# Mixer and output of a hybrid decoder trunk: another order of the pooling maps, masks and shift as matmuls, output in pairs of tiles

## The chip, the core and the metric

The kernel runs on one core of a Trainium2 chip. The metric is the device time of one execution in microseconds (us); smaller is better. Five engines run their own instruction queues in order and wait for one another by semaphores: TensorE (PE in the profile; PEld is its weight load), VectorE (DVE), ScalarE (ACT), GpSimd (POOL) and SyncE (SP), which here only issues DMA transfers. Some transfers are issued from ACT's queue.

## The reference

One step of a trunk of two layers, for a prompt of 256 tokens and eight single tokens of other requests, side by side as 264 columns of width 1024. Each layer is feed-forward, mixer, feed-forward, each followed by a layer norm.

```python
h = layer_norm(DN_ALPHA * x + 0.5 * swiglu(x, f1g, f1u, f1d), ln1_g, ln1_b)
...
h = layer_norm(DN_ALPHA * h + mix, ln2_g, ln2_b)
y = layer_norm(DN_ALPHA * h + 0.5 * swiglu(h, f2g, f2u, f2d), ln3_g, ln3_b)
```

The mixer projects h to q, k, v, z, two gate rows and pooling inputs p. One half is a gated delta rule of four heads (causal convolution of width 4 and silu on q, k, v; decays as exp of differences of running sums, masked to the causal half; a triangular solve). The other half takes trailing means over 2, 4, 8 and 16 positions of four groups p(0) to p(3), minus the token, times a 128x128 matrix for each group. Outputs are the last hidden state and the new states.

## The kernel before

The hidden state X lies in SBUF as eight tiles of 128 features by 264 columns. Every large product is made of three matmuls for each of 8 slices (`mm3`, L217): each number is split into a rounded part and a rest, so weights exist as `whi` (ACT, L178) and `wlo` (DVE, L183, one instruction of 128x1024 for each product), and the state as HH and HL, or, before its norm is known, RH and RL. A product of 24 matmuls fills one 128x264 tile.

The order on PE is the order in which the code is written. On the other engines a scheduler orders the instructions, guided by `tc.high_priority()` and `behind(...)`. The in-order queue that results is what counts.

**Norms.** Class `Norm` (L239) sums X and its squares tile by tile on POOL or DVE (`acc`). `stats` (L337) makes mean and variance by four f32 matmuls `ps`; `normalise` (L357) subtracts and scales X in pairs of tiles. So that PE need not wait, `raw_products` (L401) first computes products of the unnormalised state (four k products `pk` in the mixer, six products in a feed-forward) with `stats` between them; `settle` corrects them afterwards (`fa`).

**Mixer, first part** (L495 on). After the four k products come `pba` (the two gate rows) together with the products q0 and p3, then `pbt` (transposes of the gates). DVE turns the gates into `bat`, a chain of small 128x12 instructions (L655 to L671), then `gm` (four 128x512 instructions, L702), which PE turns into `pdiff`, ACT into the decays `DT`, and POOL masks (L710, L711). Three functions make tiles: `q_tile` and `v_tile` (a product, then `conv`: one ACT and three DVE instructions `c`) and `p_tile` (L590: a product, a copy into `ext`, and on POOL g+1 sums `wsum`). `p_map(g)` (L609) makes the means `dm` by four DVE instructions, the last of them L620, and its `finish` the matmul `py` and a split into RH and RL. The order of these on PE is written out by hand: q1, p2, q2, p1, `py` of map 3, q3, the six `pdiff`, p0, `py` of map 2, v0, `py` of map 1, v1, v2, `py` of map 0, a mean (`centre`), v3.

`ext` and `wsum` have two buffers each, `dm` shares four buffers with others.

**Mixer, second part.** From `pP` on PE runs the levels of the triangular solve, with the decode tokens' state products `psk` and other work as fillers. `decode_conv` (L776) works on POOL and ACT; `less_shift` (L324) then subtracts a mean from all eight X tiles on POOL; `stack(0, ...)` (L902) makes `parts` on POOL (L906), which PE transposes (`pst`, L908). `s_read` (L854) scales the decode states S by their decay on POOL (L885). At last `w_pool` adds the output projection (`pop`, `pout`) to X.

**End.** `output` (L379) normalises the eight tiles on DVE, POOL and ACT, and SP writes them out.

Of the kernel before, what the change touches and what calls it, by code (L numbers as in the profile page):

```python
# [34 lines left out]
SB = 3  # L35
IDLE = 18
# [53 lines left out]
def trunk(ctx: ExitStack, tc: tile.TileContext, a: dict):  # L90
# [17 lines left out]
    gto = cpool.tile([P, 2, P], F32R, name="gto")  # L108

# [129 lines left out]
    class Norm:  # L239
# [52 lines left out]
        def add_scaled(self, m, ps, scale):  # L292
            y = X[:, m, :]
            if m >= 2:
                nc.vector.tensor_add(y, ps, y)
                self.shifted(m, nc.gpsimd, nc.gpsimd)
# [82 lines left out]
        def output(self, out):  # L379
            for m in (0, 1, 2, 3, 6, 7, 4, 5):  # L380
                y = X[:, m, :]
                (nc.gpsimd if m > 3 else nc.vector).tensor_sub(y, y, self.dmu)
            prev = None
            for m in (0, 1, 2, 3, 6, 4, 5, 7):
                y = X[:, m, :]
                if m > 5:
                    nc.gpsimd.tensor_mul(y, y, self.rstd)
                    with behind(prev):
                        nc.scalar.activation(y, y, AF.Identity, scale=self.g(m), bias=self.b(m))
                else:  # L390
                    nc.vector.scalar_tensor_tensor(y, y, self.g(m), self.rstd, ALU.mult, ALU.mult)
                    if m > 3:
                        nc.vector.tensor_scalar(y, y, self.b(m), None, ALU.add)
                    else:
                        prev = nc.scalar.activation(y, y, AF.Identity, bias=self.b(m))
                n = {4: 0, 6: 0, 5: 2, 7: 2}.get(m, 1)
                if n:
                    nc.sync.dma_start(out=out[(m - n + 1) * P:(m + 1) * P, :].rearrange("(m p) t -> p m t", p=P),
                                      in_=X[:, m - n + 1:m + 1, :])
# [28 lines left out]
    def ffn(src, norm, xnext, late=False):  # L428
        with tc.tile_pool(name="fp", bufs=1, reuse_waits="tile") as fp:
# [16 lines left out]
            if src is not None:  # L446
                W.ahead(6)
                raw = src.raw_products("gugugu", [((0,), 0, 6), ((1,), 0, 6), ((2,), 0, 6), None, ((3,), 0, 6),
# [46 lines left out]
    def mixer(l, src, norm, xstack):  # L495
        with tc.tile_pool(name="mp", bufs=1, reuse_waits="tile") as mp:
# [39 lines left out]
            def k_raw(ps):  # L536
                y, bias = src.settle(ps)
                raw = mp.tile([P, T], F32, name="raw", tag="tmp", bufs=4)
                nc.scalar.activation(raw, y, AF.Identity, bias=bias)
                return raw  # L540
# [5 lines left out]
            pk_ = src.raw_products("kkkk", [((0,), 0, 7), ((1,), 0, 7), None, ((0, 1), 7, KD), ((2,), 0, KD), ((3,), 0, KD)])  # L546
# [6 lines left out]
            pq, pp, pba = (psa.tile([P, T], F32, name=n, tag="ax") for n in ("pq", "pp", "pba"))  # L553
            for k in range(KD):
                nc.tensor.matmul(pba, wb[:, k, :], HH[:, k, :], start=k == 0, stop=False)
                nc.tensor.matmul(pba, wb[:, k, :], HL[:, k, :], start=False, stop=k == KD - 1)
                mm3(pq, wq, k, HH[:, k, :], HL[:, k, :], k == 0, k == KD - 1)
                mm3(pp, wp, k, HH[:, k, :], HL[:, k, :], k == 0, k == KD - 1)
            xstack.close()
# [6 lines left out]
            def q_tile(j, ps=None):  # L566
                W.ahead(2)
# [41 lines left out]
            def p_map(g):  # L609
                ext, smp, cur = pend[g]  # L610
                wd = 2 << g
                dm = mp.tile([P, T], F32, name="dm", tag="tmp", bufs=4)
# [9 lines left out]
                def finish():  # L622
                    py = psa.tile([P, T], F32, name="py", tag="ax")
                    nc.tensor.matmul(py, pw[:, g, :], dm, start=True, stop=True)
                    yp = mp.tile([P, T], F32, name="yp", tag="tmp", bufs=4)
# [5 lines left out]
            bar = mp.tile([8, 3 * P], F32, name="bar")  # L631
            nc.gpsimd.memset(bar[:, T:], 1.0)
            with tc.high_priority():
                nc.scalar.activation(bar[:, :T], pba[32:40], AF.Copy)
                nc.vector.tensor_add(bar[:, :T], pba[0:8], bar[:, :T])
            q_tile(0, pq)
            p_tile(3, pp)
            for j in range(4):
                conv(kr[j], j)
            ck = ct[0:4]  # L640

            pbt = psa.tile([P, 3, 8], F32, name="pbt", tag="ax")
            for t in range(3):
                nc.tensor.transpose(pbt[:, t, :], bar[:, t * P:(t + 1) * P], ident(8))
# [39 lines left out]

            q_tile(1)
            p_tile(2)
            q_tile(2)
            map3 = p_map(3)
# [3 lines left out]
            map2 = p_map(2)  # L692

# [4 lines left out]
            with tc.high_priority():  # L698
                for t in range(2):
                    for i in range(2):  # L700
                        gm = gms[t, i] = mp2.tile([P, H, P], F32R, name="gm", tag=f"{'TU'[t]}{i}")
                        nc.vector.tensor_mul(gm, lemask, gp[:, i, t, :].unsqueeze(2).to_broadcast([P, H, P]))  # L702
            for j, (t, msk) in enumerate(((0, gto[:, 1]), (1, gto[:, 0]), (1, gto[:, 1]))):
                pd = psa.tile([P, H, P], F32, name="pdiff", tag="ax")
                for i in range(2):
                    nc.tensor.matmul(pd, msk, gms[t, i], start=i == 0, stop=i == 1)
                dt = DT[:, :, j * P:(j + 1) * P]
                e_last = nc.scalar.activation(dt, pd, AF.Exp)
# [5 lines left out]
            p_tile(0)  # L714
            map2()
            v_tile(0, e_last)
            p_map(1)()
# [21 lines left out]
            for t in range(2):  # L739
                sumsq(ck, ssk, ke, t)  # L740
            v_tile(2, e_last)
# [4 lines left out]
            p_map(0)()  # L746
# [18 lines left out]

            state = {}
# [9 lines left out]
            def decode_conv():  # L776
# [9 lines left out]
                state["dsq"] = nc.gpsimd.tensor_mul(dsq[:, 8:12], dec[:, 0:4], dec[:, 4:8])  # L786
# [58 lines left out]
            skt = mp.tile([P, T], F32, name="skt", tag="tmp", bufs=4)[:, 0:P]  # L845
# [8 lines left out]
            def s_read(x):  # L854
# [18 lines left out]
                def last():  # L873
# [28 lines left out]
            def stack(i, src_, dst):  # L902
# [3 lines left out]
                nc.gpsimd.tensor_sub(pt[:, :, 2 - i, :], hb(src_), pt[:, :, 0, :])  # L906
                p = psa.tile([P, P], F32, name="pst", tag="ax")
# [47 lines left out]
            def w_pool(m):  # L955
# [6 lines left out]
                def step(k):  # L962
                    mm3(ps, w, 4 * (m % 2) + k, mh[4 + k], ml[4 + k], k == 0, k == 3)
# [108 lines left out]
            norm.less_shift(state["dsq"])  # L1072
# [15 lines left out]
            def stack_u():  # L1088
                stack(1, us, ust)
# [3 lines left out]
            def w_level():  # L1093
# [4 lines left out]
                       lambda: z_level(2, lambda: stack(0, dk, kst), s_read(1), nothing),  # L1098
# [179 lines left out]
    def constants_in():  # L1278
        nc.sync.dma_start(out=sm, in_=a["small"])
        nc.sync.dma_start(out=cst, in_=a["cst"])  # L1280
        nc.scalar.activation(onr, cst[:, C_M1024:C_M1024 + P], AF.Copy)
        nc.scalar.activation(gto, cst[:, C_ONE:C_ONE + 2 * P].rearrange("p (i n) -> p i n", i=2), AF.Copy)
# [107 lines left out]
```

## Time and profile before

| | |
|---|---|
| median of 3 runs | 1085.35 us (1083.95 to 1085.57) |
| profiled execution | 1089.43 us, of which the span is 1087.6 us |
| PE busy | 1046.0 us, 96% |
| DVE busy | 765.6 us, 70% |
| ACT busy | 581.8 us, 53% |
| POOL busy | 205.9 us, 19% |
| mean granted TensorE clock | 0.989 |

The profile shows one execution. Its shares are means over two feed-forwards and a mixer in each layer, which have different limits. A row of the waits view gives who waits on PE, for whom, the sum, how many times and the longest. A timeline row gives start, duration, engine, line, what is written and read, the count, and in brackets the idle time before it and who ended that. A duration contains the start-up of an instruction; the distance of two starts is what a queue advances.

### The profile page before, as it was taken

The numbers are of one execution on the slowest core, as the hardware profiler recorded it, in microseconds if no ns is written. First come the engines' busy times: TensorE is split into PE (matmuls) and PEld (weight loads), VectorE is DVE, ScalarE is ACT, GpSimd is POOL, SyncE is SP. The second block draws the span as 40 slices with busy tenths as digits, with TensorE's granted clock in tenths as the row PEclk, the third lists the DMA queues.
The fourth block names the chain that finished last, engine by engine and source line by source line (L and its number), as shares of the span: only waits on it lengthen the run. The fifth ranks groups of instructions, "written<-read, shape, count | busy, mean of one in ns | idle before, by whom it ended". The sixth has DMA issues, their size and how long they took to land.

```text
span 1087.6 us, 20766 instructions
## 1 busy us (share of the span) xinstructions
PE 1046.0 (96%) x8410; PEld 1030.9 (95%) x8410; DVE 765.6 (70%) x1226; ACT 581.8 (53%) x1016; POOL 205.9 (19%) x248
## 2 busy tenths in 40 slices
PE   8999999998899999999999999999899999999995
PEld 8999999988798999999999999999788999999994
DVE  5555567899789955557785555778996898555554
ACT  6444445666447744444574444466664476444432
POOL 0000012244940000003200000322467300000132
PEclk9999999999999999999999999999999999999997
DMA  8554444732234355544725545565331345455441
GB/s 306 187 192 172 179 172 184 290 130 83 97 133 169 127 190 189 194 169 180 265 86 194 179 172 192 180 236 195 130 119 41 154 165 188 166 190 194 155 156 40
DMA packets 35872, 183.24 MB, mean 168 GB/s; under 512 B 6848, under 2 KB 12608, under 8 KB 15552
## 3 DMA queue, kind: packets, MB, share of 16 engines
q1 hardware_dynamic: 28704, 175.19, 44.6%
q10 hardware_dynamic: 7072, 6.72, 1.8%
q8 instruction: 66, 1.08, 0.4%
q14 instruction: 30, 0.25, 0.1%
HBM read 175.18 MB, written 6.72 MB: 167 GB/s over the span
## 4 chain that ended last, share of the span: by engine, by line
PE 82%; DVE 10%; ACT 3%; POOL 2%; issue 1%; DMA 1%; ACTq 0%; DVEq 0%
PE pd L219 8%; PE pd L221 8%; PE pd L220 8%; PE pu L220 8%; PE pu L219 8%; PE pu L221 8%; PE pg L220 7%; PE pg L219 7%; PE pg L221 7%; DVE wlo L183 2%; POOL X L327 1%; DVE c L525 1%; ACT X L367 1%; DMA wraw<-in_f_gu 1%; PE pout L220 1%
## 5 line engine op out<-in xcount | busy, mean ns | idle before, releaser
L183 DVE TENSOR_TENSOR wlo<-wraw,whi 128x1024 fp32r<-128x1024 f32 (+1 forms) x301 | 369.9, 1231 | 203.8 <-ACT whi L178 203.0
L178 ACT ACTIVATE whi<-wraw 128x1024 fp32r<-128x1024 f32 (+1 forms) x301 | 312.5, 1041 | 318.7 <-issue 116.9
L219 PE MATMUL pd<-gh,whi 128*128 128x264 f32 x704 | 200.6, 285 | 0.0
L221 PE MATMUL pd<-gh,wlo 128*128 128x264 f32 x704 | 200.2, 284 | 0.0
L220 PE MATMUL pd<-gl,whi 128*128 128x264 f32 x704 | 199.1, 283 | 0.0
L219 PE MATMUL pg<-HH,whi 128*128 128x264 f32 x632 | 179.8, 284 | 1.2 <-ACT whi L178 1.2
L221 PE MATMUL pg<-HH,wlo 128*128 128x264 f32 x632 | 179.6, 284 | 0.3 <-DVE wlo L183 0.3
L219 PE MATMUL pu<-HH,whi 128*128 128x264 f32 x632 | 179.5, 284 | 0.0
L220 PE MATMUL pg<-HL,whi 128*128 128x264 f32 x632 | 179.4, 284 | 0.0
L220 PE MATMUL pu<-HL,whi 128*128 128x264 f32 x632 | 179.2, 284 | 0.0
L221 PE MATMUL pu<-HH,wlo 128*128 128x264 f32 x632 | 179.2, 284 | 0.0
L220 PEld LDWEIGHTS pd<-gl,whi 128*128 128x128 f32 x704 | 132.6, 188 | 0.0
L221 PEld LDWEIGHTS pd<-gh,wlo 128*128 128x128 f32 x704 | 132.6, 188 | 0.0
L219 PEld LDWEIGHTS pd<-gh,whi 128*128 128x128 f32 x704 | 132.5, 188 | 0.0
L301 POOL TENSOR_TENSOR s<-X 128x264 fp32r<-128x264 f32 x4 | 3.0, 759 | 632.7 <-DVE X L298 632.7
L219 PEld LDWEIGHTS pg<-HH,whi 128*128 128x128 f32 x632 | 119.1, 188 | 1.5 <-ACT whi L178 1.4
L221 PEld LDWEIGHTS pg<-HH,wlo 128*128 128x128 f32 x632 | 118.6, 188 | 0.9 <-DVE wlo L183 0.7
L220 PEld LDWEIGHTS pg<-HL,whi 128*128 128x128 f32 x632 | 119.2, 189 | 0.1
L220 PEld LDWEIGHTS pu<-HL,whi 128*128 128x128 f32 x632 | 119.2, 189 | 0.0
L219 PEld LDWEIGHTS pu<-HH,whi 128*128 128x128 f32 x632 | 119.1, 189 | 0.0
L221 PEld LDWEIGHTS pu<-HH,wlo 128*128 128x128 f32 x632 | 118.5, 188 | 0.0
L439 DVE TENSOR_TENSOR gt<-sg,pu 128x264 f32<-128x264 f32 x79 | 33.9, 429 | 50.5 <-PE pu L221 50.5
(374 smaller groups left out, 2051.0 us busy)
## 6 DMA issues: line engine op xcount, KB each, us to landing
wraw<-in_f_gu SPq DMA_DIRECT2D x86, 1024.0 KB, 4.8
wraw<-in_f_d SPq DMA_DIRECT2D x44, 1024.0 KB, 4.8
wraw<-in_w_in SPq DMA_DIRECT2D x20, 1024.0 KB, 5.0
wraw<-in_w_out SPq DMA_DIRECT2D x8, 1024.0 KB, 4.8
S<-in_sdelta SPq DMA_DIRECT2D x8, 512.0 KB, 6.2
out_o_ds<-S ACTq DMA_DIRECT2D x8, 512.0 KB, 2.6
X<-in_xT ACTq DMA_DIRECT2D x4, 264.0 KB, 5.4
wraw<-in_f_gu SPq DMA_DIRECT2D x4, 256.0 KB, 7.1
```

The costliest lines, as they stand in the source:

```text
L178: self.last_hi = nc.scalar.activation(h, r, AF.Copy)
L183: nc.vector.tensor_sub(l, r, h.bitcast(F32))
L219: nc.tensor.matmul(ps, hi[:, k, :], xh, start=first, stop=False)
L220: nc.tensor.matmul(ps, hi[:, k, :], xl, start=False, stop=False)
L221: nc.tensor.matmul(ps, lo[:, k, :], xh, start=False, stop=last)
L301: nc.gpsimd.tensor_add(self.s2, X[:, 0, :], X[:, 1, :])
L327: nc.gpsimd.tensor_sub(X[:, m, :], X[:, m, :], self.shift)
L367: nc.scalar.activation(X[:, m, :], X[:, m, :], AF.Identity, scale=self.g(m), bias=self.b(m))
L439: nc.vector.tensor_mul(gt, sg, u)
L525: nc.vector.scalar_tensor_tensor(c[:, d:SEQ], y[:, 0:SEQ - d], cw(j, 3 - d), c[:, d:SEQ], ALU.mult, ALU.add)
```

## The change

It has seven parts.

1. In `add_scaled` the last tile's instructions get high priority.
2. `stats` stands one product earlier in the mixer's `raw_products`, and one product later in the second feed-forward's (`late`).
3. `pba` runs beside q0 alone, and p3 follows; `pbt` is placed inside p3.
4. The convolutions of the four k products are spread between the q and p products, and the maps take another place: p0 is computed before `pdiff`, map 1 after v1, map 0 after v3. `dm` gets two buffers of its own.
5. POOL's masks on `DT` are replaced by matmuls that add a large negative number (`far`) above the diagonal, and by two further `pdiff` matmuls.
6. `less_shift` becomes a matmul of one row in each `pop` product; `parts` for `stack(0, ...)` is made right in `decode_conv`; S is scaled on ACT, in 128x128 pieces.
7. `output` works on pairs of tiles, reads the mean from PSUM on DVE, and issues four transfers instead of six.

```diff
@@ add_scaled
+                with tc.high_priority() if m == KD - 1 else nullcontext():
+                    nc.vector.tensor_add(y, ps, y)
+                    self.shifted(m, nc.gpsimd, nc.gpsimd)
@@ centre, less_shift
-            self.set_shift(p, 4.0)
-        def less_shift(self, after):
-            for m in range(KD):
-                with behind(after):
-                    nc.gpsimd.tensor_sub(X[:, m, :], X[:, m, :], self.shift)
+            self.less = lpool.tile([P, T], F32R, name="less", tag="shift")[0:1]
+            nc.scalar.activation(self.less, p[0:1], AF.Copy, scale=-4.0 * ALPHA)
+        def less_shift(self, ps):
+            nc.tensor.matmul(ps, gto[0:1, 0], self.less, start=True, stop=False)
@@ output
-            for m in (0, 1, 2, 3, 6, 7, 4, 5):
...
+            for n, y in enumerate(pairs):
+                if n < 3:
+                    nc.vector.tensor_sub(y, y, by2(self.mean))
+                else:
+                    for m in (6, 7):
+                        nc.gpsimd.tensor_sub(X[:, m, :], X[:, m, :], self.dmu)
+            for n, y in enumerate(pairs):
+                nc.vector.tensor_mul(y, y, by2(self.rstd))
+                for m in (2 * n, 2 * n + 1):
+                    if n < 3:
+                        nc.scalar.activation(X[:, m, :], X[:, m, :], AF.Identity, scale=self.g(m), bias=self.b(m))
+                    else:
+                        nc.vector.tensor_scalar(X[:, m, :], X[:, m, :], self.g(m), self.b(m), ALU.mult, ALU.add)
+                nc.sync.dma_start(out=out[2 * n * P:2 * (n + 1) * P, :].rearrange("(m p) t -> p m t", p=P), in_=y)
@@ raw_products of ffn (late) and of mixer
-  [((0,), 0, 6), ((1,), 0, 6), ((2,), 0, 6), None, ((3,), 0, 6),
+  [((0,), 0, 6), ((1,), 0, 6), ((2,), 0, 6), ((3,), 0, 6), None,
-  [((0,), 0, 7), ((1,), 0, 7), None, ((0, 1), 7, KD), ((2,), 0, KD), ((3,), 0, KD)]
+  [((0,), 0, 7), None, ((1,), 0, 7), ((0, 1), 7, KD), ((2,), 0, KD), ((3,), 0, KD)]
@@ mixer, order of the maps
+            conv(kr[0], 0)
             q_tile(1)
+            conv(kr[1], 1)
             p_tile(2)
+            conv(kr[2], 2)
             q_tile(2)
+            conv(kr[3], 3)
             map3 = p_map(3)
             p_tile(1)
             map3()
             q_tile(3)
             map2 = p_map(2)
+            p_tile(0)
@@ pdiff
+                steps = [(msk, gms[t, i]) for i in range(2)]
+                if j == 1:
+                    steps += [(gto[:, 1], gms[0, i][:, :, P - 1:P].to_broadcast([P, H, P])) for i in range(2)]
+                else:
+                    steps.append((far, upper))
-                if j != 1:
-                    nc.gpsimd.tensor_mul(dt, dt, lemask)
-            nc.gpsimd.tensor_mul(DT[:, :, P:2 * P], DT[:, :, P:2 * P], DT[:, :, P - 1:P].to_broadcast([P, H, P]))
@@ decode_conv, s_read, w_pool
+                in_parts(0, dk)
-                        s = Ss[h][:, 4 * x:4 * x + 4, :]
-                        nc.gpsimd.tensor_mul(s, s, ab[:, h * NB + 4 * x:h * NB + 4 * x + 4].unsqueeze(2)
-                                             .to_broadcast([P, 4, P]))
+                        for b in range(4 * x, 4 * x + 4):
+                            s = Ss[h][:, b, :]
+                            nc.scalar.activation(s, s, AF.Copy, scale=ab[:, h * NB + b:h * NB + b + 1])
+                    if k == 0:
+                        norm.less_shift(ps)
-            norm.less_shift(state["dsq"])
```

**DVE, first mixer, from the gate chain to map 3.** `dm_2869` before and `dm_2881` in the change are the means of map 3, `dm_2956` and `dm_2968` those of map 2; `gm` feeds `pdiff`. Before:

```order
L619 TENSOR_TENSOR dm_2869<-wsum_2689,cst_72 128x16
L669 SCALAR_TENSOR_TENSOR xa_2724<-p__2728,xa_2724 128x12
L183 TENSOR_TENSOR wlo_2877<-wraw_2874,whi_2876 128x1024
L671 TENSOR_TENSOR gg_2748<-xa_2724,nega_2721 128x12
L620 TENSOR_TENSOR dm_2869<-dm_2869,ext_2677 128x16
L183 TENSOR_TENSOR wlo_2879<-wraw_2874,whi_2878 128x1024
L702 TENSOR_TENSOR gm_2962<-cst_72,gp_2752 128x512
L702 TENSOR_TENSOR gm_2966<-cst_72,gp_2752 128x512
```

In the change:

```order
L708 TENSOR_TENSOR gm_3009<-cst_72,gp_2740 128x512
L708 TENSOR_TENSOR gm_3013<-cst_72,gp_2740 128x512
L526 SCALAR_TENSOR_TENSOR c6_2869<-pq_2844,sm_73,c6_2869 128x254
L526 SCALAR_TENSOR_TENSOR c3_2875<-raw_2586,sm_73,c3_2875 128x253
L526 SCALAR_TENSOR_TENSOR c6_2869<-pq_2844,sm_73,c6_2869 128x253
L628 SCALAR_TENSOR_TENSOR dm_2881<-wsum_2705,ext_2693 128x8
L630 TENSOR_TENSOR dm_2881<-wsum_2705,cst_72 128x16
L185 TENSOR_TENSOR wlo_2930<-wraw_2927,whi_2929 128x1024
L626 SCALAR_TENSOR_TENSOR dm_2968<-wsum_2826,ext_2791 128x240
L628 SCALAR_TENSOR_TENSOR dm_2968<-wsum_2826,ext_2791 128x8
L630 TENSOR_TENSOR dm_2968<-wsum_2826,cst_72 128x16
L631 TENSOR_TENSOR dm_2881<-dm_2881,ext_2693 128x16
```

The last instruction of map 3 (L620, now L631) stood ahead of all four `gm`; now it stands behind them, behind one more `wlo` and behind three instructions of map 2. In both versions PE's `py` of map 3 stands between the products p1 and q3.

**PE, first mixer, the matmuls of `pdiff` in the change.** Before there were six, right behind q3; in the change p0 is ahead of them.

```order
L718 MATMUL pdiff_3015<-gm_3007,gto_80 128x512
L718 MATMUL pdiff_3015<-gm_3009,gto_80 128x512
L718 MATMUL pdiff_3015<-gto_80,far_81 128x512
L718 MATMUL pdiff_3020<-gm_3011,gto_80 128x512
L718 MATMUL pdiff_3020<-gm_3013,gto_80 128x512
L718 MATMUL pdiff_3020<-gm_3007,gto_80 128x512
L718 MATMUL pdiff_3020<-gm_3009,gto_80 128x512
L718 MATMUL pdiff_3026<-gm_3011,gto_80 128x512
L718 MATMUL pdiff_3026<-gm_3013,gto_80 128x512
L718 MATMUL pdiff_3026<-gto_80,far_81 128x512
L635 MATMUL py_3040<-dm_2968,pw_2395 128x264
```

Ten matmuls stand where six stood, and no POOL instruction follows them.

**POOL, first mixer, after the decode convolution.** Before:

```order
L781 TENSOR_TENSOR dsq_3265<-dec_3264 128x64
L786 TENSOR_TENSOR dsq_3265<-dec_3264 128x32
L327 TENSOR_TENSOR X_74<-X_74,shift_3200 128x264
L785 TENSOR_TENSOR kq_81<-dec_3264,kq_81 128x4x16
L327 TENSOR_TENSOR X_74<-X_74,shift_3200 128x264 x7
L1008 TENSOR_TENSOR N_3441<-MT_3202,cst_72 128x128 x2
L1008 TENSOR_TENSOR N_3444<-MT_3202,cst_72 128x128 x2
L906 TENSOR_TENSOR parts0_82<-dec_3264,parts0_82 128x4x8
L885 TENSOR_TENSOR S0_3279<-S0_3279,ab_3267 128x512
```

In the change:

```order
L790 TENSOR_TENSOR dsq_3268<-dec_3267 128x64
L796 TENSOR_TENSOR dsq_3268<-dec_3267 128x32
L1022 TENSOR_TENSOR N_3438<-MT_3199,cst_72 128x128 x2
L794 TENSOR_TENSOR kq_82<-dec_3267,kq_82 128x4x16
L916 TENSOR_TENSOR parts0_83<-dec_3267,parts0_83 128x4x8
L1022 TENSOR_TENSOR N_3441<-MT_3199,cst_72 128x128 x2
L1022 TENSOR_TENSOR N_3536<-MT_3199,cst_72 128x128 x2
```

The eight X instructions between `dsq` and `parts` are gone, and S is no longer touched here.

## Rows read from the trace of the kernel before

**Rows 1.** Waits of PE over the whole span: who waits, for whom, total, times, longest.
```profile
PE py L624 <- DVE dm L620: 6.2, 2, 3.2
PE pst L908 <- POOL parts L906: 5.6, 2, 2.8
PE ps L341 <- DVE acc L281: 2.8, 2, 1.4
PE pdiff L706 <- DVE gm L702: 2.1, 2, 1.2
...
PE pba L556 <- DVE HL L377: 1.3, 2, 0.7
...
PE pba L555 <- ACT HH L369: 1.2, 2, 0.6
PE pp L221 <- DVE wlo L183: 1.2, 2, 0.6
...
PE psk L861 <- DVE RL L851: 1.0, 3, 0.4
```

**Rows 2.** Windows, first mixer: length, busy PE, PEld, DVE, ACT, POOL, PEclk, DMA.
```profile
240.00:247.00 7.00, 5.73 (x37) 4.86 (x37) 7.00 (x15) 6.19 (x13) 5.11 (x4) 1.00 0.32 123
...
253.00:258.00 5.00, 5.00 (x29) 4.93 (x29) 4.41 (x10) 3.28 (x6) 0.00 (x0) 0.66 0.00 0
...
285.00:288.00 3.00, 3.00 (x15) 3.00 (x15) 0.53 (x2) 0.28 (x1) 3.00 (x4) 0.50 0.00 0
```

**Rows 3.** Timeline of PE, first mixer: start, duration, instruction, idle before.
```profile
226.14 0.28 PE L219 MATMUL pp<-HH,whi 128*128 128x264 f32 x1
...
229.04 0.28 PE L219 MATMUL pq<-HH,whi 128*128 128x264 f32 x1
...
236.40 0.68 PE L624 MATMUL py<-dm,pw 128*128 128x264 f32 x2 [0.26 <-PE pp L221]
...
253.07 0.48 PE L219 MATMUL pv<-HH,whi 128*128 128x264 f32 x1
...
257.73 1.03 PE L729 MATMUL psq<-cst,c 128*128 128x128 f32 x8
...
267.74 1.04 PE L1013 MATMUL pP<-cst,MT 128*128 128x128 f32 x8
```

**Rows 4.** Timeline of DVE, first mixer, from the gates to the last step of map 2.
```profile
223.24 0.18 DVE L647 COPY bat<-pbt 128x24 f32<-128x24 f32 x1
...
231.46 0.46 DVE L525 SCALAR_TENSOR_TENSOR c<-pq,sm,c 128x254 f32<-128x254 f32 x1
231.85 0.15 DVE L666 SCALAR_TENSOR_TENSOR p__2728<-p__2728,y__2727 128x12 f32<-128x12 f32 x1
231.93 1.21 DVE L183 TENSOR_TENSOR wlo<-wraw,whi 128x1024 fp32r<-128x1024 f32 x1
...
242.11 0.83 DVE L620 TENSOR_TENSOR dm<-dm,ext 128x16 f32<-128x16 f32 x1
```

**Rows 5.** Timeline of POOL, first mixer: sums for map 2.
```profile
230.66 0.85 POOL L604 TENSOR_TENSOR wsum<-ext 128x398 f32<-128x398 f32 x1 [3.43 <-issue]
234.40 3.73 POOL L604 TENSOR_TENSOR wsum<-wsum 128x396 f32<-128x396 f32 x2 [2.89 <-DVE xa L669]
```

**Rows 6.** Timeline of DVE and PE around the statistics, first mixer.
```profile
204.11 0.60 DVE L283 TENSOR_TENSOR acc<-acc,sq 128x264 f32<-128x264 f32 x1
...
205.10 0.61 PE L341 MATMUL ps<-acc,cst 128*128 128x264 f32 x2
```

**Rows 7.** Timeline of DVE, second feed-forward of the first layer: the variance.
```profile
355.97 0.43 DVE L352 SCALAR_TENSOR_TENSOR var<-ps,m 128x264 f32<-128x264 f32 x1
```

**Rows 8.** Timeline of DVE, ACT and SP at the end of the kernel.
```profile
1079.01 0.43 DVE L130 SCALAR_TENSOR_TENSOR rstd<-lnv,rstd 128x264 f32<-128x264 f32 x1
...
1082.62 1.09 ACT L389 ACTIVATE X<-X,sm 128x264 f32<-128x264 f32 x2
...
1080.55 3.88 SPq L398 DMA_DIRECT2D out_o_y<-X  x6
```

More of the change, by code (lines that the diff above doesn't have):

```diff
@@ L108, in trunk @@
     gto = cpool.tile([P, 2, P], F32R, name="gto")
+    far = cpool.tile([P, P], F32R, name="far")
     kq = cpool.tile([P, H * P], F32R, name="kq")
@@ L379, in output @@
         def output(self, out):
-            for m in (0, 1, 2, 3, 6, 7, 4, 5):
[L381 to L389, printed above, removed]
-                else:
-                    nc.vector.scalar_tensor_tensor(y, y, self.g(m), self.rstd, ALU.mult, ALU.mult)
-                    if m > 3:
-                        nc.vector.tensor_scalar(y, y, self.b(m), None, ALU.add)
-                    else:
[L395 to L399, printed above, removed]
+            by2 = lambda v: v.unsqueeze(1).to_broadcast([P, 2, T])
+            pairs = [X[:, m:m + 2, :] for m in range(0, KD, 2)]
+            for n, y in enumerate(pairs):
+                if n < 3:
+                    nc.vector.tensor_sub(y, y, by2(self.mean))
+                else:
+                    for m in (6, 7):
[5 more added lines that the diff above has]
+                        nc.scalar.activation(X[:, m, :], X[:, m, :], AF.Identity, scale=self.g(m), bias=self.b(m))
+                    else:
+                        nc.vector.tensor_scalar(X[:, m, :], X[:, m, :], self.g(m), self.b(m), ALU.mult, ALU.add)
+                nc.sync.dma_start(out=out[2 * n * P:2 * (n + 1) * P, :].rearrange("(m p) t -> p m t", p=P), in_=y)
         def raw_products(self, nms, steps):
@@ L537, in k_raw @@
                 y, bias = src.settle(ps)
-                raw = mp.tile([P, T], F32, name="raw", tag="tmp", bufs=4)
+                raw = lpool.tile([P, T], F32, name="raw", tag="sq", bufs=4)
                 nc.scalar.activation(raw, y, AF.Identity, bias=bias)
@@ L552, in mixer @@
             wq, wp = W.get(), W.get()
-            pq, pp, pba = (psa.tile([P, T], F32, name=n, tag="ax") for n in ("pq", "pp", "pba"))
+            pq, pba, pp = (psa.tile([P, T], F32, name=n, tag="ax") for n in ("pq", "pba", "pp"))
             for k in range(KD):
@@ L557, in mixer @@
                 mm3(pq, wq, k, HH[:, k, :], HL[:, k, :], k == 0, k == KD - 1)
+            bar = mp.tile([8, 3 * P], F32, name="bar")
+            nc.gpsimd.memset(bar[:, T:], 1.0)
+            with tc.high_priority():
+                nc.scalar.activation(bar[:, :T], pba[32:40], AF.Copy)
+                nc.vector.tensor_add(bar[:, :T], pba[0:8], bar[:, :T])
+            pbt = psa.tile([P, 3, 8], F32, name="pbt", tag="ax")
+            for k in range(KD):
                 mm3(pp, wp, k, HH[:, k, :], HL[:, k, :], k == 0, k == KD - 1)
+                if k == 4:
+                    for t in range(3):
+                        nc.tensor.transpose(pbt[:, t, :], bar[:, t * P:(t + 1) * P], ident(8))
             xstack.close()
@@ L566, in q_tile @@
             def q_tile(j, ps=None):
-                W.ahead(2)
+                W.ahead(4)
                 conv(ps or product(W.get(), "q"), 4 + j)
@@ L611, in p_map @@
                 wd = 2 << g
-                dm = mp.tile([P, T], F32, name="dm", tag="tmp", bufs=4)
+                dm = mp.tile([P, T], F32, name="dm", tag="dm", bufs=2)
                 csm = cur[:, 15 + SEQ:].rearrange("p (b i) -> p b i", i=16)
@@ L629, in p_map @@
                 return finish
[L631 to L635, printed above, removed]
             q_tile(0, pq)
             p_tile(3, pp)
[L638 to L644, printed above, removed]
             with tc.high_priority():
@@ L844, in mixer @@
             sk = dtile("sk", 2 * HB)
-            skt = mp.tile([P, T], F32, name="skt", tag="tmp", bufs=4)[:, 0:P]
+            skt = lpool.tile([P, T], F32, name="skt", tag="sq", bufs=4)[:, 0:P]
             def s_split(h, x):
```

38 lines of the change are left out of this document (21 added, 17 removed).

## The prediction

> **What bounds the kernel now.** I read the shares first, then the waits of PE, the windows, and the timelines of the stretches where PE waits. PE is busy 96% of the span, so outside the mixers only PE's own work counts, and nothing there changes but the place of one set of statistics. What can be won lies in PE's waits [rows 1]; the listed ones sum to some 21 us of the whole execution. They come in equal pairs, one for each layer. The largest sit in the mixer: `py` waits for the last step of a map (`dm`, 6.2 us), `pst` for POOL's `parts` (5.6), `pdiff` for `gm` (2.1), the gate products for HH and HL (2.5). Behind the two longest waits the clock falls: after the wait at `py`, v1 takes 4.66 us from 253.07 to 257.73 [rows 3] with a mean granted clock of 0.66, and after the wait at `pst` the clock stands at 0.50 [rows 2], which is 1.2 GHz instead of 2.4. A product at full clock takes 2.90 us (226.14 to 229.04) [rows 3], so the first fall costs 1.7 us and the second some 1.4 us.
>
> Why `py` and `pdiff` wait is told by DVE: it is busy 7.00 of 7.00 us from 240 to 247 [rows 2]. In this stretch the queue of DVE is the limit, and PE waits for whatever stands late in it. The order on DVE therefore decides what the change does.
>
> **Prices.** From the distance of starts, a convolution step costs DVE 0.39 us, a 128x12 step 0.08; a `wlo` lasts 1.2 [rows 4].
>
> **1. High priority of the last tile.** The queues of ACT and DVE in front of the mixer hold the same instructions in the same order as before. Cost and gain 0.
>
> **2. Statistics.** In the mixer PE would reach them 21 matmuls earlier: 205.10 - 2.6 = 202.5 us. Their second sum is ready only at 204.11 + 0.60 = 204.7 [rows 6], so PE waits about 1.8 us there (0.4 of the 2.2 is filled by the first pair of matmuls, which has its data). It then reaches the gate products about 1 us later than now, when HH and HL are mostly there, so that the two waits of 0.6 and 0.7 [rows 1] go. One wait is swapped for another: 0, between -1 and +0.5. In the second feed-forward the sum is late now (1.4 us in each layer [rows 1]); one product later that wait is gone, but the variance starts at 355.97 [rows 7] behind two weight instructions on DVE, whatever PE does. PE arrives 1.4 us earlier at tiles that are not earlier. I take half of it: -0.6 in each layer, between 0 and -1.4.
>
> **3. Gates.** The gate products with q0 and p3 are 64 matmuls of 0.12 us in any order. From about 214.4 they end at 222.3; the transposes hide inside p3, so q1 starts near 222.65, half a microsecond earlier than now, and `bat` is on DVE near 221.6 rather than 223.24 [rows 4]. Its gain of 0.5 is in the sum below.
>
> **4. Order of the maps, the step that decides.** PE still asks for map 3 between p1 and q3, four products behind q1: 222.65 + 4 x 2.93 = 234.4 us. DVE now finishes map 3 behind the four `gm`, one more `wlo` and three steps of map 2. Before, from `bat` to the last step of map 2 at 242.11 it took 18.9 us [rows 4], which held 11 convolution steps, four `wlo` and four `gm`. Now 17 convolution steps lie in it, since those of the k products were moved behind `bat`: 6 x 0.39 = 2.3 more. The steps of map 2 (0.5) move behind. That gives 221.6 + 18.9 - 0.5 + 2.3 = 242.3 for map 3's third step. Less time is lost to POOL in it, since two of the seven sums and all the masks fall away: an estimate of 1.1 us, so 241.2. Then come the fifth `wlo` and, on POOL, the last two sums of map 2, which need the buffer that map 3 has just released. A sum alone takes 0.85 us, but two took 3.73 us while DVE was full [rows 5]. Taking 2 x 0.87 plus 1.2 one after the other, and 0.57 for the last four steps, map 3 is done at 244.7. Bounds: 241.8, with the sums hidden entirely and POOL's loss halved, to 246.7, with the sums at 3.73 beside the `wlo` and the loss as before. **PE idles about 10.3 us** (7.4 to 12.3) where it idles 0.3 us now, and afterwards I add the same 1.7 us of slow clock as behind the present wait [rows 2, 3].
>
> The Trainium skill ("SBUF — State Buffer", section "Who interferes with whom") states that a DVE instruction with two SBUF inputs and a GpSimd instruction that reads SBUF exclude each other for the whole instruction. The stretched sums agree with it. By that rule the `wlo` and the two sums add up, as taken; if they ran side by side, map 3 would be done 1.1 us earlier and the whole kernel 2.3 us faster than I forecast.
>
> Behind that, DVE has 10 us of lead: q3, p0, ten `pdiff` (2.6 us; now six), map 2, v0, v1, map 1, v2, map 0 and v3 find their operands. Now PE takes 31.3 us from `py` of map 3 at 236.40 to `pP` at 267.74 [rows 3]. In it lie 1.25 and 3.25 us of idle time [rows 1], 1.7 of slow clock, and about 0.7 in which matmuls drain and restart around the two waits: 24.4 us of work are left. With 0.95 for four more `pdiff` and 1.7 of slow clock behind the new wait these are 27.0, so `pP` starts at 244.7 + 27.0 = 271.7, **4.0 us later** than now. (The waits at p1 and the gates lie ahead of `py` and are in its 236.40.)
>
> **5 and 6. Masks, shift, `parts`, S.** POOL no longer has eight subtractions ahead of `parts`, so `pst` does not wait: -2.8 [rows 1], with 0.25 of restart and 1.4 of slow clock [rows 2]. S leaves POOL's queue for ACT, and the waits at `psk`, 0.5 a layer [rows 1], go with their slower matmuls, 0.3. The shift costs eight matmuls of one row at 0.12 us: +1.0. ACT gets 32 pieces of S, at about a quarter of a microsecond each; it has half of its time free in this stretch, so nothing. The output tail of the mixer loses some 0.3 us of waiting. Together **-4.5** (bounds -2 and -5.5). A mixer is thus 4.5 - 4.0 = 0.5 us faster.
>
> **7. Output.** The last ACT instruction starts before 1082.62 + 1.09 = 1083.7, and SP issues the last transfer by 1084.4 [rows 8]. The variance root now starts behind two pair instructions instead of three single ones that share time with POOL, and is ready about 1 us earlier than 1079.4 [rows 8]; then four pair products of 0.62 and six ACT instructions end near 1081.6. Gain 2.0, between 0.5 and 2.6. The extra constant at the start costs at most 0.3 on ACT, taken as 0.
>
> **Sum.** 2 x (-0.5) - 2 x 0.6 - 2.0 = -4.2. The profiled execution of 1089.43 us would become 1085.2; against the median of 1085.35, which is 4.1 us lower, 1081.2.
>
> **Rivals.** (a) **Map 3 is later still.** DVE's order is fixed, but its pace with POOL's sums isn't: at the bound of 246.7, or beyond if the slow clock lasts longer after an idle time of 10 us than after 3, each mixer loses 2 to 5 us more, which gives 1085 to 1091. The kernel is slower than before by more than 2.2 us where map 3 and the slow clock together cost 3.2 us more than taken, as with map 3 done at 248. For it: PE's wait is three times as long as any in the profile, so what follows it is not shown. Against: the sums are the only ones then running. (b) **The wait at map 3 is short**, if `gm` and the sums come without loss, or DVE starts its share of the k convolutions early enough. With 3 us of idle and no fall of the clock each mixer gains 7.3 + 1.7 = 9 us more: 1063. Against it: DVE has no idle time in this stretch [rows 2] and gets more to do in front of map 3. (c) **Waits are only exchanged**: S on ACT delays a weight part or a copy that PE needs by some 2 us a mixer, and the end of the output is set by the transfers: 1084 to 1087. For it: ACT's queue is in order and 32 pieces are 8 us.
>
> **Chances.** My forecast 0.55, (a) 0.17, (b) 0.08, (c) 0.20. Its own range is 1077 to 1084. The range to hold 8 in 10 goes from 1071 to 1088. About 0.2% (2.2 us) is what can be told from no change: faster by more than that 0.62, within it 0.20, slower 0.18, with (a) and (c) split at their ends.
>
> **What would show it.** `py` of map 3 waits for DVE's last `dm` step about 10 us in each mixer, and a stretch at half clock follows; the waits at `py` of map 1, `pdiff` and `pst` are gone; a new wait of some 1.8 us stands at the mixer's `ps`, and the one of the second feed-forward is gone; `pP` starts about 4 us later than now, counted from the k products, and the section after it is 4.5 us shorter. The prediction is wrong if the wait at `py` is below 6 or above 13 us, or if new waits for ACT appear behind `pP`.

## The result, and the profile after

The changed kernel takes 1093.98 us, median of four runs (1092.91 to 1095.10). The four runs of the kernel before beside them gave 1084.65; the ratio is 1.0089 with an interval of 1.0070 to 1.0108. It is **slower**, by less than 1%, where 1081.2 and a gain were forecast. The kernel before was timed 49 more times beside the experiments, not counting one disturbed run of 1451.30 us at a mean granted clock of 0.654: all 53 runs lie between 1082.45 and 1094.34 us, with a median of 1088.05, and 52 of them are faster than the fastest run of the change. Against that median the change costs 5.9 us (1093.98 / 1088.05 = 1.0055). The profiled executions are 1089.43 us before and 1093.62 after.

The waits of PE after (who waits, for whom, total, times, longest), to be read beside [rows 1]:

```profile
PE py L635 <- issue: 21.1, 2, 10.6
PE ps L346 <- DVE acc L285: 2.8, 2, 1.4
...
PE psk L871 <- DVE RL L861: 0.9, 2, 0.4
...
PE pu L223 <- DVE wlo L185: 0.8, 2, 0.4
PE pg L222 <- DVE HL L381: 0.7, 2, 0.4
...
PE psc L759 <- ACT QW L1063: 0.4, 2, 0.2
```

The waits at `pst`, `pdiff`, p1 and the gates are gone, and so is the one of map 1. In their place stands one wait of 10.6 us in each mixer, at `py` of map 3. The row at `ps` is now that of the mixers; before it was that of the second feed-forwards. "Issue" as its releaser is the view's inference; who was late is told by DVE's timeline of the first mixer after:

```profile
221.60 0.18 DVE L647 COPY bat<-pbt 128x24 f32<-128x24 f32 x1 [0.20 <-PE pbt L569]
...
241.22 0.15 DVE L628 SCALAR_TENSOR_TENSOR dm<-wsum,ext 128x8 f32<-128x8 f32 x1
241.30 0.16 DVE L630 TENSOR_TENSOR dm<-wsum,cst 128x16 f32<-128x16 f32 x1
241.38 1.20 DVE L185 TENSOR_TENSOR wlo<-wraw,whi 128x1024 fp32r<-128x1024 f32 x1
244.25 0.41 DVE L626 SCALAR_TENSOR_TENSOR dm<-wsum,ext 128x240 f32<-128x240 f32 x1 [1.66 <-POOL wsum L615]
244.57 0.17 DVE L628 SCALAR_TENSOR_TENSOR dm<-wsum,ext 128x8 f32<-128x8 f32 x1
244.66 0.17 DVE L630 TENSOR_TENSOR dm<-wsum,cst 128x16 f32<-128x16 f32 x1
244.74 0.17 DVE L631 TENSOR_TENSOR dm<-dm,ext 128x16 f32<-128x16 f32 x1
```

POOL in the same stretch, and PE (the first `pP` was at 267.74 in [rows 3]):

```profile
241.60 2.62 POOL L615 TENSOR_TENSOR wsum<-wsum 128x396 f32<-128x396 f32 x2 [10.07 <-DVE dm L630]
```

```profile
245.01 1.22 PE L635 MATMUL py<-dm,pw 128*128 128x264 f32 x2 [10.57 <-issue]
...
272.14 1.04 PE L1027 MATMUL pP<-cst,MT 128*128 128x128 f32 x8
...
285.65 0.27 PE L920 MATMUL pst<-cst,parts 128*128 128x128 f32 x1
...
329.70 0.29 PE L223 MATMUL pop<-RH,wlo 128*128 128x264 f32 x1
329.92 0.38 PE L331 MATMUL pop<-less,gto 1*128 1x264 f32 x1
330.24 0.39 PE L221 MATMUL pop<-RH,whi 128*128 128x264 f32 x1
330.46 0.28 PE L222 MATMUL pop<-RL,whi 128*128 128x264 f32 x1
```

The last step of map 3 is the 244.74 row: behind a `wlo`, behind POOL's two sums, behind three steps of map 2. The rows of `pop` show a second cost. Between ordinary matmuls of a product the starts lie 0.12 us apart; from 329.70 over the one-row matmul to 330.46 they lie 0.22, 0.32 and 0.22 apart, 0.76 in place of the 0.24 that the two neighbours alone would take. The weight loads (PEld) show a part of it:

```profile
329.58 0.19 PEld L223 LDWEIGHTS pop<-RH,wlo 128*128 128x128 f32 x1
329.92 0.18 PEld L331 LDWEIGHTS pop<-less,gto 1*128 1x128 f32 x1
330.23 0.19 PEld L221 LDWEIGHTS pop<-RH,whi 128*128 128x128 f32 x1
```

The ordinary load at 329.58 starts 0.12 us ahead of its matmul (329.70). The load of the one-row matmul starts with its matmul (329.92), and the load behind it only 0.01 ahead of its own (330.24): neither runs ahead as the ordinary ones do.

A window of the first mixer after (columns as in [rows 2]) shows the half clock behind the long wait, and the end of the kernel the shorter output:

```profile
244.00:250.00 6.00, 4.99 (x24) 4.81 (x25) 2.98 (x13) 1.48 (x4) 2.14 (x5) 0.58 0.14 38
```

```profile
1080.62 0.43 DVE L356 SCALAR_TENSOR_TENSOR var<-ps,m 128x264 f32<-128x264 f32 x1 [1.45 <-PE ps L349]
...
1083.62 0.43 DVE L132 SCALAR_TENSOR_TENSOR rstd<-lnv,rstd 128x264 f32<-128x264 f32 x1
...
1084.83 3.10 ACT L397 ACTIVATE X<-X,sm 128x264 f32<-128x264 f32 x6 [2.86 <-DVE X L394]
...
1085.96 2.44 SPq L400 DMA_DIRECT2D out_o_y<-X  x4
```

By stage, from starts on PE's timelines of the two profiled executions (before to after, and the difference in us; `pba` is the first gate matmul, `pop` the first output product, `pout` the last kind of output product, `pg` the first product of the next feed-forward):

| stage | mixer 1 | mixer 2 |
|---|---|---|
| up to `pba` (statistics), in mixer 2 from the layer's first `pg` | 213.43 to 214.43: +1.0 | 206.65 to 207.55: +0.9 |
| `pba` to `pP` | 54.31 to 57.71: +3.4 | 53.71 to 57.76: +4.1 |
| `pP` to `pop` | 32.28 to 28.32: -4.0 | 31.89 to 28.32: -3.6 |
| `pop` to `pout` | 32.25 to 35.98: +3.7 | 32.26 to 36.00: +3.7 |
| `pout` to `pg` | 13.00 to 11.90: -1.1 | 13.00 to 11.90: -1.1 |

The second feed-forwards become 0.4 us shorter each. From the last matmul of the statistics to the end of the span it takes 14.0 us before (1073.58 to 1087.6) and 11.9 after (1079.87 to 1091.8).

### The profile page after: what moved, and what is told of

It reads as the page before. It is cut to its first block, busy times and chain, and to the rows that moved or that the text cites. A ratio compares the mean times of both kernels' runs of the same rounds, so it can differ in the third digit from the quotient of the medians.

```text
span 1091.8 us, 20807 instructions
## 1 busy us (share of the span) xinstructions
PE 1050.5 (96%) x8434; PEld 1033.1 (95%) x8434; DVE 751.9 (69%) x1223; ACT 596.9 (55%) x1081; POOL 158.2 (14%) x206
## 4 chain that ended last, share of the span: by engine, by line
PE 87%; DVE 5%; issue 3%; ACT 3%; DMA 2%; SPq 0%; ACTq 0%; DVEq 0%
PE pd L221 7%; PE pd L223 7%; PE pd L222 7%; PE pu L223 7%; PE pu L222 7%; PE pu L221 7%; PE pg L222 7%; PE pg L221 7%; PE pg L223 7%; ACT S L896 1%; DVE xlo L185 1%; PE pop L221 1%; DMA wba<-in_w_ba 1%; PE pq L221 1%; PE pq L222 1%
```

## The experiments

**Theory** after the result: three things. PE waits for map 3, since the four DVE steps stand late in the queue; the shift's one-row matmuls cost far more than 0.12 us; and the profiled execution of the kernel before was not a typical one. **Rivals**: DVE is simply full, so another order only moves the wait; the cost at `pop` belongs to any foreign matmul in a product; the spread of the times is drift of the chip.

The experiments ran in three groups of four, each group on another chip. At a mean clock of 0.990 a straight line through times and clocks of the kernel before gives 1087.8, 1087.3 and 1087.6 us on the three. By this estimate a difference below some 0.5 us between kernels of different groups says nothing. The kernel with both edits, with which the later ones are compared, was timed in the first group only.

### The kernel before, again

No edit.

> The kernel before, unchanged. The profiled execution shown for it took 1089.4 us, its timed ones a median of 1084.7; that of the changed kernel lies with its timed ones. Theory A: that execution was 4 to 5 us longer than usual, and a second profile takes 1084 to 1086 us; the missing time shows as waits of PE or as a slower start. Theory B: the profile lengthens this kernel, and it takes 1089 again.

Measured: ten runs, 1082.27 to 1090.99, median 1089.50 (ratio 1.0001, 0.9972 to 1.0030); the profiled one, which is among them, 1090.91. Neither theory: the times, profiled or not, go with the mean granted clock that each run lists. Of the 35 runs of this kernel in that comparison:

```
clock 0.993 to 0.995   10 runs   1082.3 to 1084.6 us
clock 0.989 to 0.992   14 runs   1086.4 to 1089.9 us
clock 0.984 to 0.988   11 runs   1090.4 to 1094.3 us
```

So 0.01 of mean clock goes with some 10 us. The execution of 1089.43 us, from which [rows 1 to 6] were read, was therefore no exception: it had clock 0.989 and half clock behind all four idle stretches of about 3 us (two at `py`, two at `pst`); the three runs whose median stood ahead of the prediction (1083.95 to 1085.57) lie in and just above the first group, though more than two thirds of the runs are slower than that. All four runs of the change list 0.985 to 0.988.

The execution profiled here (clock 0.987) has half clock behind the same four stretches, but the falls differ in length. A window behind the first wait at `py`, in the first profile and in this one:

```profile
252.00:260.00 8.00, 7.25 (x46) 7.22 (x47) 6.59 (x18) 5.52 (x13) 0.00 (x0) 0.79 0.13 32
```

```profile
252.00:260.00 8.00, 6.94 (x35) 6.76 (x35) 5.72 (x17) 4.42 (x10) 0.12 (x1) 0.57 0.10 27
```

No execution near 0.995 of this kernel was profiled, so which of the falls are absent in the fast runs is inferred from their mean clock.

### The shift on 128 rows

```diff
-            self.less = lpool.tile([P, T], F32R, name="less", tag="shift")[0:1]
-            nc.scalar.activation(self.less, p[0:1], AF.Copy, scale=-4.0 * ALPHA)
+            self.less = lpool.tile([P, T], F32R, name="less", tag="shift")
+            nc.scalar.activation(self.less, p, AF.Copy, scale=-32.0 * ALPHA)
...
-            nc.tensor.matmul(ps, gto[0:1, 0], self.less, start=True, stop=False)
+            nc.tensor.matmul(ps, onr, self.less, start=True, stop=False)
```

> The changed kernel with the shift's matmul on all 128 rows (a 128x128 constant times a 128x264 tile) in place of one row. Theory: in the changed kernel each of the 16 one-row matmuls takes 0.3 us to the next start, and the matmul behind it 0.23 instead of 0.12, with 0.1 more in front, some 0.4 to 0.5 over an ordinary one. If that comes from the one-row shape, the stretch from the first output product to the last is 3 us shorter in each mixer, and the kernel 5 to 6.5 us faster than the change. Rival: the cost belongs to any change of operands between two kinds of product, and less than 1 us comes back.

Measured: 1089.82 us (1089.29 to 1090.94), 4.2 less than the change; ratio to before 1.0031 (1.0014 to 1.0048). Its timelines of PE and PEld:

```profile
332.25 0.37 PE L331 MATMUL pop<-less,onr 128*128 128x264 f32 x1
332.45 0.28 PE L221 MATMUL pop<-RH,whi 128*128 128x264 f32 x1
332.57 0.28 PE L222 MATMUL pop<-RL,whi 128*128 128x264 f32 x1
```

```profile
332.33 0.19 PEld L221 LDWEIGHTS pop<-RH,whi 128*128 128x128 f32 x1
```

The load behind the shift's matmul runs 0.12 us ahead of its own matmul (332.45) again.

From `pop` to `pout` the first mixer takes 33.59 us, against 35.98 in the change and 32.25 before: eight matmuls cost 1.3 us with 128 rows, and 3.7 with one. The clock is nearly the same in both (0.985 to 0.987 here, 0.985 to 0.988 in the change). The theory holds; its size, 5 to 6.5 us, was somewhat too large.

### Map 3 first

```diff
-                with tc.high_priority() if g < 3 else nullcontext():
+                with tc.high_priority():
```

> The changed kernel with high priority for map 3 as well, which puts its four DVE steps ahead of the second half of the gate chain. Theory: the wait of 10.6 us at py of map 3 is gone in each mixer, with 1.7 us of slow clock behind it; nothing else is late, so 20 to 24 us faster than the change, 1070 to 1074 us. Rival: DVE has the same work to do by then, and PE waits for gm or weight parts instead; half of it or less comes back, above 1082 us.

Measured: 1081.33 us (1079.55 to 1082.63), 12.7 less than the change; ratio to before 0.9939 (0.9919 to 0.9959). PE's waits in it:

```profile
PE pdiff L718 <- DVE gm L708: 5.8, 2, 2.9
PE pq L223 <- DVE wlo L185: 3.3, 2, 1.7
PE ps L346 <- DVE acc L285: 3.1, 2, 1.7
```

The wait of 21.1 is gone, but 9.1 us of others stand there instead, at `gm` and at a weight part of q3. The gain is little more than half of the 20 to 24 us expected, and the time lies between theory and rival: the place in the queue made the long wait, and DVE, busy 6.00 of 6.00 us from 234 to 240, still has too much in front of `gm`. The mean clock rises to 0.992 to 0.995.

### Both edits

The last two edits in one kernel.

> Both edits together. If the two are independent, the gains add: 26 to 30 us faster than the change, 1064 to 1069 us. If the wait at map 3 hides nothing of the second part, the stretch behind pP is as long as in the kernel with the 128-row shift alone.

Measured: 1076.28 us (1076.12 to 1076.64), 17.7 less than the change; the two gains add (4.2 + 12.7 = 16.9), though the 26 to 30 expected are missed by as much as the second edit had missed. Ratio to before 0.9905 (0.9880 to 0.9931). It **beats both kernels**, and its runs agree within 0.5 us, so the next ones take parts out of this kernel.

Its trace settles something about the clock. The same wait for `gm` stands in both mixers, and the windows behind the two differ:

```profile
245.69 0.51 PE L718 MATMUL pdiff<-gm,gto 128*128 128x512 f32 x1 [2.90 <-DVE gm L708]
...
773.62 0.50 PE L718 MATMUL pdiff<-gm,gto 128*128 128x512 f32 x1 [2.90 <-DVE gm L708]
```

```profile
246.00:252.00 6.00, 6.00 (x29) 5.22 (x28) 6.00 (x13) 4.27 (x8) 0.00 (x0) 0.72 0.30 94
774.00:780.00 6.00, 6.00 (x43) 5.62 (x42) 6.00 (x14) 5.21 (x11) 0.00 (x0) 1.00 0.31 100
```

Behind 2.90 us of idle time the clock falls in the first mixer and stays in the second, in one execution.

### The old output

The function `output` of the kernel before in the kernel with both edits.

> The kernel with both edits (128-row shift, map 3 first; 1076.3 us) and the output of the kernel before. The prediction gave the output by pairs 2.0 us, between 0.5 and 2.6. If that holds, 1078.3 us; if the last transfers set the end in both forms, within 0.5 us of 1076.3.

Measured: 1078.41 us (1078.36 to 1078.50), +2.1. The output by pairs is worth what was forecast; the two profiles before and after gave the same, 14.0 against 11.9 us.

### The old places of the statistics

```diff
-  [((0,), 0, 6), ((1,), 0, 6), ((2,), 0, 6), ((3,), 0, 6), None,
+  [((0,), 0, 6), ((1,), 0, 6), ((2,), 0, 6), None, ((3,), 0, 6),
...
-  [((0,), 0, 7), None, ((1,), 0, 7), ((0, 1), 7, KD), ((2,), 0, KD), ((3,), 0, KD)]
+  [((0,), 0, 7), ((1,), 0, 7), None, ((0, 1), 7, KD), ((2,), 0, KD), ((3,), 0, KD)]
```

> The kernel with both edits, and the statistics back in their places of before, in the mixers and the second feed-forwards. The prediction: nothing in the mixers (a wait of 1.4 us at the sums against two of 0.6 at HH and HL), 0.6 us lost in each second feed-forward, so 1077.5 us. Rival: the new wait in the mixer costs what the feed-forward gains, 1076.3 us; or the mixer's DVE work, which is late anyway, hides the place of the sums, and only the feed-forward's 1.4 us shows, 1079 us.

Measured: 1077.00 us (1076.66 to 1077.34), +0.7, of +1.2 forecast. The waits at HH and HL and at the feed-forward's sums come back, the mixer's at the sums goes: mostly an exchange. At the same time the waits for `gm` and for q3's weight part shrink from 9.1 to 7.3 us, so this kernel hides part of the cost. The +0.7 is also barely above what can be told between groups.

### S on POOL

```diff
-                        for b in range(4 * x, 4 * x + 4):
-                            s = Ss[h][:, b, :]
-                            nc.scalar.activation(s, s, AF.Copy, scale=ab[:, h * NB + b:h * NB + b + 1])
+                        s = Ss[h][:, 4 * x:4 * x + 4, :]
+                        nc.gpsimd.tensor_mul(s, s, ab[:, h * NB + 4 * x:h * NB + 4 * x + 4].unsqueeze(2)
+                                             .to_broadcast([P, 4, P]))
```

> The kernel with both edits, and S scaled on POOL in four columns at a time, as before. The prediction took the move to ACT as free and the gain of the second part as coming from the shift and the early parts. If so, 1076 to 1077 us, with the small wait of psc for ACT gone and the waits at psk as they are. Rival: on POOL the scaling again stretches DVE's reads of S, and psk waits more: 1078 us or above.

Measured: 1076.93 us (1076.22 to 1077.78), +0.6, within the spread of its own runs: no difference is shown. The move to ACT is close to free, as taken.

### The k convolutions behind `gm`

```diff
-            conv(kr[2], 2)
-            conv(kr[3], 3)
...
+            conv(kr[2], 2, gm_op)
+            conv(kr[3], 3, gm_op)
```

The third argument holds the three DVE steps of `conv` behind the last `gm` by `behind(...)`; the calls stand behind `pdiff`.

> The kernel with both edits, and the DVE steps of the convolutions of k products 2 and 3 held back until gm is made. In the kernel with both edits PE waits 2.9 us for gm and 1.7 us for a weight part in each mixer while DVE is full. Theory: the order on DVE decides, six steps of 0.39 us less in front of gm give 1 to 2.3 us in each mixer: 1072 to 1074 us. Rival: DVE only does other work first, or PE waits later for the k convolutions; 1076 us.

Measured: 1073.01 us (1072.83 to 1075.18), 3.3 less than with both edits (one of its four runs, 1075.18, only 1.1 less); ratio to before 0.9852 (0.9830 to 0.9874), the **best kernel of this study**. Its waits:

```profile
PE pq L223 <- DVE wlo L185: 2.3, 2, 1.2
PE psq L737 <- ACT c L534: 1.9, 2, 0.9
```

Of the 5.8 us at `pdiff` 0.4 are left; PE waits 1.9 us for the k convolutions later. The order on DVE decides, with a part of the rival.

### Parts early in the kernel before

```diff
+                in_parts(0, dk)
                 state["dsq"] = nc.gpsimd.tensor_mul(dsq[:, 8:12], dec[:, 0:4], dec[:, 4:8])
...
-            def stack(i, src_, dst):
+            def in_parts(i, src_):
...
+            def stack(i, dst):
...
```

The function `stack` is cut in two: `in_parts` makes `parts`, and what is left of `stack` transposes it.

> The kernel before, with the parts of the decode keys made in the decode convolution, ahead of six of the eight X instructions on POOL. Theory: the times of the kernel before spread from 1082 to 1094 us because TensorE's clock falls to half behind some of its four idle stretches of about 3 us and not behind others; runs at a mean clock of 0.995 take 1082 us, runs at 0.987 take 1091. With the two stretches at pst gone there are two left: 2 x 2.8 = 5.6 us less in the fastest runs, 1076 to 1077 us, a spread of about 5 us in place of 10, and a median near 1080. Rival: the clock falls for another reason; the spread stays 10 us and only the 5.6 us come off.

Measured: 1083.12 us (1081.62 to 1084.61), ratio to before 0.9949 (0.9930 to 0.9967). The spread falls to 3 us, in the theory's direction (5 expected), but the fastest runs gain only some 1 us, and the median is 3 us above the 1080 expected. Two reasons are in its profile: the wait at `pst` is gone, while those at `psk` grow from 1.0 to 1.9 us, and those at `py` from 6.2 to 7.2, with the clock at 0.990 to 0.993 in every run. In the profiled run half clock follows `py` in both mixers; by the clock it does so in nearly all of these runs, where it came in some before.

### The shift on 32 rows

```diff
+            nc.scalar.activation(self.less, p[0:32], AF.Copy, scale=-128.0 * ALPHA)
...
+            nc.tensor.matmul(ps, onr[0:32], self.less, start=True, stop=False)
```

> The kernel with both edits (1076.3 us), the shift's matmul on 32 rows in place of 128. The one-row form cost 4.2 us more than the 128-row one. If any change of the number of rows between matmuls costs that, 1080 to 1081 us; if a single row is the cause, 1076.3 us.

Measured: 1081.24 us (1079.86 to 1081.92), 5.0 above the same kernel with 128 rows. The instructions of the tile `less` there (min, median, max in ns; then in the change, then in the change with 128 rows):

```profile
L331 PE MATMUL pop<-less,onr x16: 381/383/385, 293.9 to 857.9; 32*128 32x264 f32 x16
```

```profile
L331 PE MATMUL pop<-less,gto x16: 381/383/386, 300.5 to 870.4; 1*128 1x264 f32 x16
```

```profile
L331 PE MATMUL pop<-less,onr x16: 283/368/372, 300.4 to 865.7; 128*128 128x264 f32 x16
```

One row and 32 rows behave alike: from `pop` to `pout` the first mixer takes 36.01 us here, 35.98 with one row. So it is not the single row that costs. Both forms on a part of the rows cost the same, though the matmul itself lasts hardly longer than one of 128 rows (383 against 368 ns). The loss stands between the starts, where the weight loads are no longer ahead; why they aren't was not tested.

### Masks on POOL

The loop of `pdiff` with its masks on POOL from the kernel before, in the kernel with both edits.

> The kernel with both edits, and the masks on POOL again in place of four pdiff matmuls. The prediction counted the four matmuls at 0.95 us in each mixer and gave POOL's masks 1.1 us of DVE's time. Theory: behind gm DVE has slack in this kernel, so only the matmuls count: 1.9 us faster, 1074.4 us. Rival: POOL's masks hold up DVE's next weight parts and PE waits for them: 1077 us or more.

Measured: 1082.68 us (1082.48 to 1083.09), +6.4: the theory falls, and the rival holds for the time, but not for its cause. The wait that appears is not one for weight parts, but one of the second part:

```profile
PE pUt L1059 <- ACT V L1054: 2.8, 2, 1.4
```

From `pP` to `pop` the first mixer takes 30.54 us against 28.14, and the second the same 2.4 more: some 5 of the 6.4 us. From `pba` to `pP` the first takes 0.3 us more, and the second 2.0 more; there the clock falls behind the wait for `gm` (0.83 from 774 to 784), where it stayed in the kernel with both edits. What delays V behind the masks was not followed further.

### Parts early, and map 1 behind v1, in the kernel before

```diff
-            p_map(1)()
+            map1 = p_map(1)
...
                 sumsq(ck, ssk, ke, t)
+            map1()
...
```

The rest is the edit of the run with the parts alone.

> The kernel before with the early parts and with map 1's matmul behind v1, nothing else. Theory: all four idle stretches of about 3 us are gone, so the clock stays: 2 x (2.8 + 3.2) = 12 us less than the fastest runs of before, 1070 to 1073 us, with a spread of at most 2 us. Rival: PE waits for the weight parts of v0 or v1 instead, since DVE is full up to there: 1076 us or more.

Measured: 1077.99 us (1077.66 to 1078.71), ratio to before 0.9906 (0.9885 to 0.9927). The spread is 1 us and the clock 0.994 to 0.995 in all six runs, as the theory has it, while the kernel before beside it, in the same group, spread from 1083.55 to 1092.11: drift of the chip doesn't explain the spread. The trace shows no half clock in either mixer. The gain on the fastest runs is 4.5 us, not 10 to 12: PE waits elsewhere, as the rival has it.

```profile
PE pv L221 <- DVE wlo L183: 1.9, 2, 1.1
PE py L624 <- DVE dm L620: 1.9, 2, 0.9
PE psk L863 <- DVE RL L853: 1.6, 3, 0.7
...
PE psk L863 <- POOL kq L786: 1.4, 2, 0.7
```

## Why the prediction was wrong

The time missed the forecast by 12.8 us. Of these 5.5 are the shift's price, 1.3 the rest of parts 5 and 6, 1.4 the stretch up to `pP`, 0.4 the second feed-forwards, and 4.1 the step from the profiled execution to the median of three runs; what is left is 0.1.

**Right, close to the digit: part 4, the step that decides.** `bat` at 221.6 was forecast and measured; map 3 at 244.7 against 244.9; PE's idle time 10.3 against 10.6; `pP` at 271.7 against 272.1; half clock behind the wait. In the second mixer the stage from `pba` to `pP` cost some 0.6 more than in the first. The edit that moves the late steps forward gives 12.7 us back, so this wait is the largest cost of the change, and it had been priced.

The Trainium skill ("SBUF — State Buffer", section "Who interferes with whom") says that a DVE instruction with two SBUF inputs and a GpSimd one that reads SBUF exclude each other. By that rule the `wlo` and POOL's two sums were added up. The trace agrees: the sums start at 241.60, the `wlo` runs until 242.58, and the two sums, 0.85 each alone [rows 5], take 2.62 us, to 244.22, which is 1.64 behind the end of the `wlo`.

**Wrong: the price of the shift in part 6, "eight matmuls of one row at 0.12 us: +1.0".** The stretch from `pop` to `pout` became 3.7 us longer in each mixer. I had taken the price of an ordinary matmul of the same number of columns for one of another shape, with no row for it, and gave it no bound of its own. The runs show 0.47 us for such a matmul between full ones, with one row or with 32. On 128 rows the same eight cost 1.3. The mis-sized term is 2.7 us in each mixer, 5.5 in all; 4.2 of them came back in the run. With it the section behind `pP` was to become 4.5 us shorter in each mixer; up to `pg` it became 1.3 and 0.9 shorter.

**Also too large: the rest of parts 5 and 6.** The wait at `pst` and its half clock went as forecast, but the waits at `psk` stayed at 0.4 us each and `psc` got a new one. `pP` to `pop` gained 4.0 and 3.6 us where 4.5 + 1.0 - 0.3 = 5.2 were forecast; the stretch behind `pout` gave some of it back, 1.1 us in each mixer where 0.3 were forecast. What the masks on matmuls are worth was mis-sized the other way: counted as a cost of 0.95 us a mixer, yet with POOL's masks the kernel with both edits is 6.4 us slower; in the change itself this was not tried.

**Wrong: the step from the profiled execution to the median.** The sum was made against an execution of 1089.43 us in which the clock fell behind all four waits of 3 us, and the difference was then taken from a median of 1085.35, which three runs gave by chance: that of the 53 is 1088.05. In the faster runs of the kernel before most of these falls don't happen, or are shorter, by their mean clock, so there is less to win by removing them: 1082.3 at clock 0.995 and 1090.9 at 0.987 are one and the same kernel. The change instead has two idle stretches of 10.6 us; behind both the clock falls in its profile, and all its runs list 0.985 to 0.988. Between profiled executions the change costs 4.2 us, against the median of 53 runs 5.9, against the four runs beside it 9.3.

**Right:** the last tile's priority does nothing to the queues (that was read, not run); the statistics are mostly an exchange (0.7 measured, 1.2 forecast; by the stages the second feed-forwards gain 0.4 each, 0.6 forecast); the output by pairs is worth 2.1 us (2.0 forecast); S on ACT is about free. Rival (a) was nearest to the time, but not by its mechanism: map 3 was not later than taken, and its 1085 to 1091 ends below the 1093.98. Rival (c) was right only in that new waits of ACT exist; they are 0.2 us each. The chance of 0.18 for slower was too low: the shift's price stood on no row, and the base on three runs and one profile.

## What to carry to other kernels

A relief for an engine that waits works only if the order on the engine it waits for is read to the last instruction: here four steps of 0.1 to 0.3 us, at the wrong place in a full queue, cost 12.7 us, and one line about their priority gives it back. A small matmul on a part of the rows wasn't small between full ones here; measure it before it replaces work that was hidden on another engine, or give it all 128 rows. And where a kernel idles TensorE for some 3 us at several places, look at the granted clock of each run before a sum is taken from one profile to a median: the spread of the runs may be the falls of the clock, and here removing the idle time removed the spread too.

## What was not expected of the hardware

- A matmul of 1 or 32 rows by 264 columns between full ones costs PE some 0.47 us (3.73 / 8) by the stretch, one of 128 rows 0.17 (1.34 / 8). In the trace with one row its weight load, and the one behind it, do not run ahead of their matmuls.
- Behind idle stretches of 2.90 us TensorE's clock falls to half (1.2 GHz) in one mixer and stays at 2.4 GHz in the other, in one execution of the kernel with both edits. The kernel before, with four stretches of 2.8 to 3.3 us, takes 1082 to 1094 us, by its mean clock. Behind 10.6 us the clock fell in both places of the change's profile, and all its runs list 0.985 to 0.988.
